# Hybrid decoder trunk on one core: where the state-space input weights are loaded and split, and when the last expert's hidden rows are turned

## The chip, the cores and the metric

One core of one Trainium2 chip runs the whole program in one launch. The metric is device time in microseconds (us), lower is better. Engines are named as in the profile: PE (TensorE matmul), PEld (its weight loads), DVE (VectorE), ACT (ScalarE), POOL (GpSimd), SP (SyncE, which only issues DMAs here).

## The reference, cut to what matters

Two layers over 512 tokens of 1024 values. Layer 0 has a mixer of sparse attention and gated linear attention, layer 1 a state-space mixer (S5); each layer ends in a norm, a mixture of 16 experts, and a second norm.

```python
for layer in range(DEPTH):                      # 2
    m = even_mixer(...) if layer % 2 == 0 else s5_mixer(h, s5_w_in, ...)
    h = layer_norm(ALPHA * h + m)
    f = hier_moe(h, ...)                        # 16 experts, 2 chosen per token
    h = layer_norm(ALPHA * h + f)

def s5_mixer(x, w_in, ...):
    u = x @ w_in                                # 512x1024 @ 1024x1024, the first thing it does
    ...
```

The change lies at the end of the experts (both layers) and, in layer 0, between there and `x @ w_in`.

## The kernel before, in words

All matmuls that need fp32 accuracy are done in three passes: an operand is split into a high part (an ACT copy to the rounded type) and a low part (a subtraction on DVE or POOL), and `mm3` (lines 103 to 108) multiplies high by high, high by low and low by high. `split` (98) makes both parts of a tile; `part` (1119 to 1126) does it for half of an expert's weight matrix.

**The experts, `Experts.run` (1279 to 1419).** An expert e has gate, up and down weights, each in two halves. PE multiplies gate, then up, then the down weights of expert e-1. The order on each engine is fixed by the code (a `manual_schedule` region with all five engines). `high()` and `low()` split the next half of the list `todo`; for e = 15 the last two of them, `(15, 4)` and `(15, 5)` (the down weights of expert 15), are split beside the up product. `hidden` (1156) applies the gate on ACT and the product on DVE; `turn_hidden` (1163) transposes the 128x512 hidden rows on PE (line 1169) and splits them into the tiles `hh` and `hl`, of which there is one buffer each. `table` (1261 to 1267) scales an expert's output on ACT and writes it to a table in DRAM (`y_d`) by a DMA that ACT issues. `fetch(i)` (1269 to 1277) is four indirect DMAs on POOL, one for each quarter of the tokens, that add rows of that table to `acc`; `fetch(1)` needs the tables up to expert 13, `fetch(0)` that of expert 14. Expert 15 goes another way: `rows` (1179) and then `combine` (1192), matmuls that place its rows, whose result DVE adds to `acc` (line 1206) once `fetch(0)` has landed.

**What is put amid the tail.** `run` gets a generator `early`. In layer 0 that is `S5.early` (1773): it loads a small table `s_gb` (the second norm's scale and shift, 2 x 1024 single values, two POOL DMAs, line 1780) and the state-space input weights `w_in`, two DMAs of 2 MB on SP's queue (line 1784), into the two `raw` buffers of the ring; this is called at e = 15, after the up product. After `fetch(0)` and `turn_hidden(15)` its second part runs `unit_in(0)` and `unit_in(1)` (1764): each splits a quarter of `w_in` in two blocks of 128x1024, ACT copy (line 100) and DVE subtraction (101). Then come the two halves of `down(15)`. In layer 1 `early` is `load_norm` (2165), two SP loads into a buffer that the last up product has to free; its later parts are empty.

**The end of the experts and the norm.** `beyond()` (1209) is a branch that is not taken here (more than 128 rows for an expert). Behind it `S5.enter` (1797) runs the norm (`closing`, 1422 to 1461) and the projection. `closing` adds each quarter (1206), squares (1435), takes the deviations, and scales quarters 0 and 1 (1459); its generator `last` does quarters 2 and 3, interleaved below, and ends in the ACT scaling at 1452. `turn(0)` transposes quarters 0 and 1 on PE (1810) and then makes for each of 8 k a high part on ACT (1815, needs `s_gb`), a difference on DVE (1817, four buffers in turn), and the low part on POOL (1819). `project((0, 1), a)` then multiplies units 0 (columns 0 to 255 of `w_in`), after that `turn(2)`, `project((2, 3), a)` with unit 1, and both again for the other half of the tokens. In this region the hand-written order holds for PE, DVE and ACT; POOL's instructions are placed by the program's own scheduler.

**What follows in `S5.mix`.** `rt.load()` (`Router.load`, 792 to 802) issues nine small POOL DMAs for the next router (`r1R`, lines 796 and 798, four of the latter; `r1rb`, 799 and 800; `r1gb`, 802 twice), and `prepare` (808) multiplies two of them on POOL. They are written behind `enter`, but POOL is not in a hand-written order there, and the scheduler puts them first behind the branch. `load_glu(0)` is 16 SP loads of 128 KB into the first `raw` buffer (line 1938), ahead of all other SP loads of the mixer, and has to wait until `unit_in(1)` has read that buffer. `put_u` (1847), `block_in(4)`, `states` and the rest follow.

Of the kernel before, what the change touches and what calls it, by code (L numbers as in the profile page):

```python
# [10 lines left out]
F32 = mybir.dt.float32  # L11
F32R = mybir.dt.float32r
# [9 lines left out]
P = 128  # L22
D = 1024
KO = D // P
# [25 lines left out]
class Ctx:  # L50
# [44 lines left out]
        self.n += 1  # L95
        return self.ring.tile([P, 4096], dt, tag="raw", name=f"raw{self.n}")[:, :n]

    def split(self, hi, lo, src):

        self.nc.scalar.activation(hi, src, AF.Copy)  # L100
        self.nc.vector.tensor_sub(lo, src, hi.bitcast(F32))  # L101

    def mm3(self, out, a, b, start, stop):

# [950 lines left out]
class Bank:  # L1055
# [17 lines left out]
    def next(self, *s):  # L1073
        self.n += 1
        return self.pair(self.pairs[(self.n - 1) % len(self.pairs)], *s)


class Experts:
# [83 lines left out]

    def turn_hidden(self, name, s):
        c = self.c
        hh = self.late.tile([P, 4, P], F32R, tag="hh", name=f"{name}hh")
        hl = self.late.tile([P, 4, P], F32R, tag="hl", name=f"{name}hl")
        ps = c.psum().rearrange("p (b t) -> p b t", b=4)
        for f in range(4):
            c.nc.tensor.transpose(ps[:, f], s.rearrange("p (q f) -> p f q", f=4)[:, f], c.ident)
        c.split(hh, hl, ps)  # L1170
        return hh, hl

    def down(self, py, h, w, half):
        for f in range(2):
            for i in range(2):
                self.c.mm3(py[i], [t[:, 2 * half + f] for t in h],
                           [t[:, i * 512:(i + 1) * 512] for t in w[f]], half + f == 0, half == 1 and f == 1)
# [101 lines left out]
    def run(self, early):  # L1279
# [34 lines left out]
        def low():  # L1314

            if lows:
                lows.pop(0)()
                load(lows.pop(0) + 6)
# [4 lines left out]
        with c.tc.manual_schedule(engines={c.nc.tensor.engine, c.nc.scalar.engine, c.nc.vector.engine,  # L1323
                                       c.nc.gpsimd.engine, c.nc.sync.engine}):
            load(0, 1)
            x = self.first_rows()
            tokens, gates = rt.slots(0, 2)
            tokens()
            nc.gpsimd.dma_start(rt.y_d[0:1, :], self.xe[0][0:1, :])
            xs = {1: gather(1)}  # L1330
            rt.early_gates()
            nc.scalar.preload_act_table(AF.Silu)
            def product(ps, raw, ks, x=x):
                for k in ks:
                    nc.tensor.matmul(ps, x[:, k], raw[:, k], start=(k == 0), stop=(k == KO - 1))  # L1335
            pg, pu = c.psum(), c.psum()
            product(pg, raws[0, 0], range(KO))
            load(2, 3)
            for _ in range(2):
                high()  # L1340
                low()
            product(pu, raws[0, 1], range(7))
            rt.gates()
            gates()
            tokens, gates = rt.slots(2, 2)
            product(pu, raws[0, 1], range(7, KO))
            load(4, 5)
            high()
            low()
            s, mul = self.hidden(f"{n}0", pg, pu)  # L1350
            mul()
            x = self.turn(f"{n}1", xs[1], [t[:, :KO] for t in self.bank.pair(2, 2 * KO, P)])
            tokens()
            xs[2] = gather(2)
            h = self.turn_hidden(f"{n}0", s)
            gates()
            high()
            low()
            self.table_rows()
            py = [c.psum(), c.psum()]  # L1360
            for i in range(2):
                self.down(py, h, parts[0, 4 + i], i)
            high()
            self.table(0, py, rt.gcol[:, 0:1])
            low()
            high()
            low()
            h = None

            def down(e, i, h):  # L1370
                if not i:
                    py[:] = [c.psum(), c.psum()]
                self.down(py, h, parts[e, 4 + i], i)
                if i and e < TABLE:
                    self.table(e, py, rt.gcol[:, e:e + 1])
                elif i:
                    ys[e] = self.rows(f"{n}{e}", py, rt.idxf[:, e:e + 1], rt.gcol[:, e:e + 1])
            for e in range(1, 16):
                pg, pu = c.psum(), c.psum()

                high()
                self.product(pg, x, parts[e, 0], 0)
                if e > 1:
                    h = self.turn_hidden(f"{n}{e - 1}", s)
                low()
                high()
                self.product(pg, x, parts[e, 1], 1)
                more = rt.slots(e + 2, 2) if e < 14 and e % 2 == 0 else ()
                low()
                s, mul = self.hidden(f"{n}{e}", pg, pu)  # L1390
                if e == 15:
                    self.fetch(1)
                for i in range(2):
                    if e > 1:
                        high()
                    self.product(pu, x, parts[e, 2 + i], i)
                    if e > 1:
                        low()
                mul()
                if e + 1 < 16:  # L1400
                    x = self.turn(f"{n}{e + 1}", xs[e + 1])
                for step in more:
                    step()
                if e + 2 < 16:
                    xs[e + 2] = gather(e + 2)
                if e == 15:
                    next(early)
                for i in range(2):
                    high()
                    if e > 1:  # L1410
                        down(e - 1, i, h)
                    low()
            self.fetch(0)
            h = self.turn_hidden(f"{n}15", s)
            next(early)
            for i in range(2):
                down(15, i, h)
        self.beyond()
        return lambda *args: self.combine([ys[15]], *args), self.xe

# [330 lines left out]
class S5:  # L1751
# [9 lines left out]
        h, l = self.bank.pair(3 + i, 4, L)  # L1761
        return [(h[:, k], l[:, k]) for k in range(4)]

    def unit_in(self, i):

        w = self.w[i] = self.bank.pair(1 + i % 2, KO, 256)
        src = self.raw[i // 2][:, :, i % 2 * 256:i % 2 * 256 + 256]
        for b in range(2):
            cols = slice(b * P, (b + 1) * P)
            self.c.split(*[t[:, :, cols].rearrange("p k (c g) -> p k c g", c=16) for t in w],  # L1770
                         src[:, :, cols].rearrange("p k (g c) -> p k c g", c=16))

    def early(self):

        c, nc = self.c, self.c.nc
        self.bank = self.get_bank()
        self.gb = self.bank.pool.tile([P, 2, KO], F32, name="s_gb")
        with nc.allow_non_contiguous_dma(reason="2048 values"):
            for i, v in enumerate((self.fn_g, self.fn_b)):
                nc.gpsimd.dma_start(self.gb[:, i], v.rearrange("(k p) -> p k", p=P))  # L1780
        self.raw, self.w = [], {}
        for i in range(2):
            t = c.raw(KO * 512).rearrange("p (k n) -> p k n", k=KO)
            nc.sync.dma_start(t, self.w_in.rearrange("(k p) n -> p k n", p=P)[:, :, i * 512:(i + 1) * 512])
            self.raw.append(t)
        yield
        self.unit_in(0)
        self.unit_in(1)
        yield

    def project(self, bs, ts, ps, ks=range(KO)):
        for k in ks:
# [4 lines left out]
    def enter(self, es, combine, free):  # L1797

        c, nc, acc = self.c, self.c.nc, self.c.acc
        with c.tc.manual_schedule(engines={nc.tensor.engine, nc.vector.engine, nc.scalar.engine}):  # L1800
            steps = closing(c, c.scope(es, "n0"), combine, free[0])
            x = self.x = self.half(0) + self.half(1)
            g, b = self.gb[:, 0], self.gb[:, 1]

# [20 lines left out]
                pass  # L1825
            ps = self.first = [c.psum() for _ in range(4)]
            self.project((0, 1), a, ps)
            b_ = turn(2)
            self.project((2, 3), a, ps)
            self.project((0, 1), b_, ps)  # L1830
# [293 lines left out]
def trunk(ctx: ExitStack, tc: tile.TileContext, x, rel_bias, ab_w_in, gla_gate_w2, gla_gate_b, gla_norm_g,  # L2124
# [3 lines left out]
    c = Ctx(tc, ctx)  # L2128
    nc = c.nc
# [4 lines left out]
    def moe(layer, mixer, early, last):  # L2134
        nonlocal bank
        es = ExitStack()
        rt = Router(c, es, ln_mix_g[layer], ln_mix_b[layer], moe_r_coarse[layer], moe_rb_coarse[layer],
                    moe_r_fine[layer], moe_rb_fine[layer], f"r{layer}")
        experts = Experts(c, rt, (moe_w_gate[layer], moe_w_up[layer], moe_w_down[layer]), f"e{layer}")
        mixer(rt, experts)  # L2140
        bank = bank or Bank(c, bank_s)
        experts.open(es, bank)
        last(es, *experts.run(early()))

    def first(rt, experts):
        su = ExitStack()
# [18 lines left out]
    def load_norm():  # L2165
        t = bank.tile(2, 2, D, dt=F32)
        for i, v in enumerate((ln_ffn_g[1], ln_ffn_b[1])):
            nc.sync.dma_start(t[:, i], bcast_row(v))
        fgb.append(t)
        yield  # L2170
        yield

    def finish(es, combine, free):
        pool, acc, (fg, fb) = c.scope(es, "n1"), c.acc, (fgb[0][:, i] for i in range(2))
# [92 lines left out]
```

## Time and profile before

| | us |
|---|---|
| three timed runs | 1344.14, 1324.39, 1338.56 (median 1338.56) |
| the profiled execution, its own time | 1330.89 |
| its span in the profile, first to last instruction | 1328.8 |
| outside the span (difference) | 2.1 |
| PE busy | 1195.4 (90%) |
| DVE busy | 1035.4 (78%) |
| ACT busy | 724.6 (55%) |
| POOL busy | 572.4 (43%) |

Times in rows are counted from the span's start. A timeline row gives start, duration, engine, line, operation, output and inputs, and in brackets how long the engine stood idle just before it and what ended that. "ACTq" and "SPq" are an engine's DMA issues. The granted clock of TensorE is given as a share of full speed.

### The profile page before, as it was taken

To read this page: it belongs to the slowest core of one execution; us is meant where nothing else is said; L and a number is where in the kernel's file an instruction comes from. 1 tells how busy PE (TensorE), PEld (TensorE's weight loads), DVE (VectorE), ACT (ScalarE), POOL (GpSimd) and SP (SyncE) were. 2 spreads that over 40 slices of the span, in tenths; PEclk is the share of its full clock that TensorE was granted. 3 is DMA by queue.
4 is the path that set the end of the run, shared out by engine and by line. 5 is a ranking of instruction groups with operands and counts; after the bars stand their busy time and mean duration, and the time that the engine had idled before them with its cause. 6 is when DMAs were issued, how large, how long until landed. Compare 5 with 4: busy or idle time off the path is not lost.

```text
span 1328.8 us, 18794 instructions
## 1 busy us (share of the span) xinstructions
PE 1195.4 (90%) x6879; PEld 954.8 (72%) x6879; DVE 1035.4 (78%) x1621; ACT 724.6 (55%) x854; POOL 572.4 (43%) x570
## 2 busy tenths in 40 slices
PE   7898798989989999999984999999988999999981
PEld 5577675567757778788864877888857787877860
DVE  5868868777578999999975567363668999999956
ACT  3443214545547777888853422332246787877842
POOL 4076934697512454455444100250002553454533
PEclk9998898999899999999996999999999999999995
DMA  9324352342379999999995788534149999999974
GB/s 229 99 74 146 108 175 73 96 133 77 110 290 333 359 382 393 359 378 409 396 281 107 219 277 267 159 127 159 48 186 338 359 394 365 383 358 405 382 213 123
DMA packets 130063, 324.56 MB, mean 244 GB/s; under 512 B 43851, under 2 KB 80995, under 8 KB 104233
## 3 DMA queue, kind: packets, MB, share of 16 engines
q1 hardware_dynamic: 106128, 285.69, 59.5%
q0 software_dynamic: 7328, 16.51, 5.3%
q10 hardware_dynamic: 16504, 21.04, 4.4%
q8 instruction: 59, 0.97, 0.3%
q14 instruction: 44, 0.35, 0.1%
HBM read 293.18 MB, written 43.49 MB: 253 GB/s over the span
## 4 chain that ended last, share of the span: by engine, by line
PE 36%; DVE 16%; DMA 14%; issue 6%; ACT 3%; POOL 1%; ACTq 0%; DVEq 0%; POOLq 0%; SPq 0%
PE ps L106 9%; DVE b L1124 9%; PE ps L107 9%; PE ps L108 9%; DMA e1xe<-r1h_d,r1idx 3%; DMA acc<-r0y_d,e0row 2%; DMA e0xe<-r0h_d,r0idx 2%; DMA acc<-r1y_d,e1row 2%; PE ps L1915 2%; ACT b L1123 2%; DMA rawd<-in_moe_w_gate_dram 2%; PE ps L167 1%; PE ps L1912 1%; PE ps L1335 1%; PE ps L940 1%
## 5 line engine op out<-in xcount | busy, mean ns | idle before, releaser
L1124 DVE TENSOR_TENSOR b<-raw,b 128x2048 fp32r<-128x2048 f32 x120 | 296.6, 2501 | 8.1 <-ACT b L1123 8.1
L1124 POOL TENSOR_TENSOR b<-rawd,b 128x2048 fp32r<-128x2048 f32 x28 | 168.4, 6015 | 204.0 <-ACT b L1123 154.8
L1123 ACT ACTIVATE b<-raw 128x2048 fp32r<-128x2048 f32 x120 | 229.7, 1918 | 35.3 <-PE ps L108 15.7
L1124 DVE TENSOR_TENSOR b<-rawd,b 128x2048 fp32r<-128x2048 f32 x36 | 160.8, 4473 | 24.0 <-ACT b L1123 23.6
L1123 ACT ACTIVATE b<-rawd 128x2048 fp32r<-128x2048 f32 x64 | 122.2, 1915 | 16.5 <-PE ps L108 7.9
L1130 POOL DMA_INDIRECT e1xe<-r1h_d,r1idx x15 | 39.5, 2636 | 64.1 <-DVE r1gcol L1051 34.7
L101 DVE TENSOR_TENSOR b<-raw,b 128x2048 fp32r<-128x2048 f32 (+1 forms) x18 | 41.3, 2312 | 32.9 <-ACT b L100 32.9
L1130 POOL DMA_INDIRECT e0xe<-r0h_d,r0idx x15 | 39.6, 2641 | 55.8 <-DVE r0gcol L1051 30.5
L107 PE MATMUL ps<-b,b 128*128 128x512 f32 (+1 forms) x160 | 56.9, 355 | 4.6 <-POOL b L1819 4.6
L106 PE MATMUL ps<-b,b 128*128 128x512 f32 (+1 forms) x160 | 57.4, 359 | 0.0
L108 PE MATMUL ps<-b,b 128*128 128x512 f32 (+1 forms) x160 | 56.7, 354 | 0.0
L106 PE MATMUL ps<-gh,b 128*128 128x512 f32 x128 | 51.2, 400 | 0.0
L107 PE MATMUL ps<-gl,b 128*128 128x512 f32 x128 | 50.1, 391 | 0.1
L108 PE MATMUL ps<-gh,b 128*128 128x512 f32 x128 | 49.8, 389 | 0.0
L603 ACT ACTIVATE lt<-lt,rmin 128x128 f32<-128x128 f32 (+3 forms) x32 | 17.9, 561 | 42.9 <-DVE rmin L601 42.9
L100 ACT ACTIVATE b<-raw 128x2048 fp32r<-128x2048 f32 (+1 forms) x18 | 34.5, 1946 | 7.2 <-DMA raw<-in_s_w_out_dram 3.7
L1864 POOL COPY s_r<-s_si 128x256 f32<-128x256 f32 x8 | 5.8, 730 | 74.2 <-DVE s_Z L1897 51.6
L107 PEld LDWEIGHTS ps<-b,b 128*128 128x128 f32 x160 | 31.5, 197 | 8.5 <-POOL b L1819 4.8
L106 PEld LDWEIGHTS ps<-b,b 128*128 128x128 f32 x160 | 31.4, 196 | 4.5 <-ACT b L1815 0.4
L108 PEld LDWEIGHTS ps<-b,b 128*128 128x128 f32 x160 | 31.4, 196 | 3.9
L670 PE MATMUL ps<-raw,oB 128*128 128x512 f32 x64 | 32.3, 629 | 0.0
L2019 POOL TENSOR_TENSOR acc<-acc,s_fg 128x1024 f32<-128x1024 f32 x4 | 12.9, 3236 | 39.6 <-DMA s_fg<-in_ln_ffn_g_dram 39.6
(1266 smaller groups left out, 3749.8 us busy)
## 6 DMA issues: line engine op xcount, KB each, us to landing
raw<-in_moe_w_up_dram SPq DMA_DIRECT2D x64, 1024.0 KB
rawd<-in_moe_w_gate_dram SPq DMA_DIRECT2D x56, 1024.0 KB
raw<-in_moe_w_down_dram SPq DMA_DIRECT2D x56, 1024.0 KB
raw<-in_moe_w_gate_dram SPq DMA_DIRECT2D x8, 1024.0 KB
rawd<-in_moe_w_down_dram SPq DMA_DIRECT2D x8, 1024.0 KB
raw<-in_s_glu_w_dram SPq DMA_DIRECT2D x64, 128.0 KB
b<-store SPq DMA_DIRECT2D x8, 1024.0 KB
s_si<-store SPq DMA_DIRECT2D x8, 770.0 KB
```

The costliest lines, as they stand in the source:

```text
L100: self.nc.scalar.activation(hi, src, AF.Copy)
L101: self.nc.vector.tensor_sub(lo, src, hi.bitcast(F32))
L106: mm(out, a[0], b[0], start=start, stop=False)
L107: mm(out, a[0], b[1], start=False, stop=False)
L108: mm(out, a[1], b[0], start=False, stop=stop)
L167: c.nc.tensor.transpose(ps[:, b], src[:, (b0 + b) * P:(b0 + b + 1) * P], c.ident)
L603: nc.scalar.activation(lt[:, :n], lt[:, :n], AF.Exp, scale=-1.0, bias=m, accum_out=self.rsum[:, h:h + 1])
L670: nc.tensor.matmul(ps, oB[:, k, tb * P:(tb + 1) * P], raw_o[1][:, k, hs], start=(k == 0), stop=(k == 3))
L1123: c.nc.scalar.activation(h, r, AF.Copy)
L1124: low = lambda: (eng or c.nc.vector).tensor_sub(l, r, h.bitcast(F32))
L1130: self.c.nc.gpsimd.indirect_dma_start(out=x, out_offset=None, in_=self.rt.h_d[:, :], in_offset=bass.IndirectOffsetOnAxis(ap=idx, axis=0), ...
L1915: nc.tensor.matmul(ps[h, j, 1:64], cw[r, i, j, h], X[b][r, i, j, 0:63], start=False, stop=True, skip_group_check=True)
```

## The change

1. `S5.early` is no generator any more and is called once, behind `fetch(0)`. It loads `w_in` on POOL's queue instead of SP's, ahead of the two `s_gb` loads. In layer 1 `load_norm` is called there too; it stays on SP.
2. `unit_in(0)` moves behind `closing` in `enter`; the subtraction of its first block goes to POOL, that of its second stays on DVE. `unit_in(1)` moves behind the first `project((0, 1), a)`.
3. POOL is put into the hand-written order of `enter`.
4. At e = 15, in both layers, the splits `(15, 4)` and `(15, 5)` move from beside the up product to beside `down(14)`, and `turn_hidden(15)` moves between the two halves of `down(14)`. `hh` and `hl` get two buffers each.

```diff
-    def split(self, hi, lo, src):
+    def split(self, hi, lo, src, engine=None):
         self.nc.scalar.activation(hi, src, AF.Copy)
-        self.nc.vector.tensor_sub(lo, src, hi.bitcast(F32))
+        (engine or self.nc.vector).tensor_sub(lo, src, hi.bitcast(F32))
...
-        hh = self.late.tile([P, 4, P], F32R, tag="hh", name=f"{name}hh")
-        hl = self.late.tile([P, 4, P], F32R, tag="hl", name=f"{name}hl")
+        hh = self.late.tile([P, 4, P], F32R, tag="hh", name=f"{name}hh", bufs=2)
+        hl = self.late.tile([P, 4, P], F32R, tag="hl", name=f"{name}hl", bufs=2)
...
                 for i in range(2):
-                    if e > 1:
+                    if 1 < e < 15:
                         high()
                     self.product(pu, x, parts[e, 2 + i], i)
...
-                if e == 15:
-                    next(early)
                 for i in range(2):
                     high()
                     if e > 1:
                         down(e - 1, i, h)
                     low()
+                    if e == 15 and not i:
+                        last = self.turn_hidden(f"{n}15", s)
             self.fetch(0)
-            h = self.turn_hidden(f"{n}15", s)
-            next(early)
+            early()
             for i in range(2):
-                down(15, i, h)
+                down(15, i, last)
...
-    def unit_in(self, i):
+    def unit_in(self, i, engines=None):
...
-                         src[:, :, cols].rearrange("p k (g c) -> p k c g", c=16))
+                         src[:, :, cols].rearrange("p k (g c) -> p k c g", c=16), engines and engines[b])
     def early(self):
         c, nc = self.c, self.c.nc
         self.bank = self.get_bank()
+        self.raw, self.w = [], {}
+        for i in range(2):
+            t = c.raw(KO * 512).rearrange("p (k n) -> p k n", k=KO)
+            nc.gpsimd.dma_start(t, self.w_in.rearrange("(k p) n -> p k n", p=P)[:, :, i * 512:(i + 1) * 512])
+            self.raw.append(t)
         self.gb = self.bank.pool.tile([P, 2, KO], F32, name="s_gb")
...
-        self.raw, self.w = [], {}
-        for i in range(2):
-            t = c.raw(KO * 512).rearrange("p (k n) -> p k n", k=KO)
-            nc.sync.dma_start(t, self.w_in.rearrange("(k p) n -> p k n", p=P)[:, :, i * 512:(i + 1) * 512])
-            self.raw.append(t)
-        yield
-        self.unit_in(0)
-        self.unit_in(1)
-        yield
...
-        with c.tc.manual_schedule(engines={nc.tensor.engine, nc.vector.engine, nc.scalar.engine}):
+        with c.tc.manual_schedule(engines={nc.tensor.engine, nc.vector.engine, nc.scalar.engine, nc.gpsimd.engine}):
             steps = closing(c, c.scope(es, "n0"), combine, free[0])
+            self.unit_in(0, (nc.gpsimd, nc.vector))
...
             self.project((0, 1), a, ps)
+            self.unit_in(1)
             b_ = turn(2)
...
-        last(es, *experts.run(early()))
+        last(es, *experts.run(early))
...
             nc.sync.dma_start(t[:, i], bcast_row(v))
         fgb.append(t)
-        yield
-        yield
```

## Rows read from the trace of the kernel before

**Rows 1.** Busy time in five stretches: columns as in the second line.
```profile
core 0: us, PE busy (x) PEld busy (x) DVE busy (x) ACT busy (x) POOL busy (x), PEclk, DMA share, GB/s
671.00:674.00 3.00, 3.00 (x15) 2.49 (x14) 3.00 (x2) 2.25 (x2) 3.00 (x1) 1.00 1.00 377
691.00:701.00 10.00, 6.41 (x16) 4.80 (x16) 1.70 (x3) 0.00 (x0) 7.64 (x5) 0.66 1.06 215
711.50:720.30 8.80, 4.08 (x17) 3.48 (x18) 5.53 (x24) 4.88 (x10) 4.68 (x15) 0.69 0.77 139
720.30:730.00 9.70, 9.70 (x63) 9.70 (x64) 3.48 (x12) 2.42 (x3) 3.97 (x7) 0.73 0.00 0
748.00:960.00 212.00, 211.21 (x1764) 170.51 (x1764) 126.08 (x194) 64.26 (x70) 34.34 (x25) 1.00 0.54 175
```

**Rows 2.** Timeline of PE, layer 0, from the first projection on.
```profile
720.30 0.58 PE L107 MATMUL ps<-b,b 128*128 128x256 f32 x1 [4.63 <-POOL b L1819]
...
728.34 1.91 PE L1810 MATMUL ps<-ident,acc 128*128 128x128 f32 x16
730.00 0.36 PE L106 MATMUL ps<-b,b 128*128 128x256 f32 x1
```

**Rows 3.** Timeline of POOL, layer 0, end of the experts to the projection.
```profile
653.74 5.77 POOL L1124 TENSOR_TENSOR b<-rawd,b 128x2048 fp32r<-128x2048 f32 x1 [9.03 <-ACT b L1123]
670.86 3.49 POOL L1274 DMA_INDIRECT acc<-r0y_d,e0row  x1 [11.35 <-DMA r0y_d<-e013y]
...
691.02 1.94 POOL L1274 DMA_INDIRECT acc<-r0y_d,e0row  x1 [8.52 <-DMA r0y_d<-e014y]
...
698.11 1.46 POOL L796 DMA_DIRECT2D r1R<-in_moe_r_coarse_dram  x1
701.38 0.94 POOL L798 DMA_DIRECT2D r1R<-in_moe_r_fine_dram  x1 [1.81 <-DMA acc<-r0y_d,e0row]
...
710.14 0.88 POOL L798 DMA_DIRECT2D r1R<-in_moe_r_fine_dram  x1 [1.68 <-DMA acc<-r0y_d,e0row]
...
713.24 0.89 POOL L802 DMA_DIRECT2D r1gb<-in_ln_mix_b_dram  x1
...
718.63 1.05 POOL L808 TENSOR_TENSOR r1R<-r1R,r1gb 128x160 f32<-128x160 f32 x2 [4.04 <-DMA r1gb<-in_ln_mix_b_dram]
719.63 4.63 POOL L1819 TENSOR_TENSOR b<-e0xe,s_gb 128x256 fp32r<-128x256 f32 x8
```

**Rows 4.** Timeline of DVE, layer 0, same stretch.
```profile
683.45 7.54 DVE L101 TENSOR_TENSOR b<-raw,b 128x1024 fp32r<-128x1024 f32 x4 [1.18 <-ACT b L100]
...
701.26 0.69 DVE L1206 CUSTOM_DVE_ANT_0 acc<-acc,ps 128x512 f32<-128x512 f32 x1 [8.56 <-DMA acc<-r0y_d,e0row]
...
707.05 0.69 DVE L1206 CUSTOM_DVE_ANT_0 acc<-acc,ps 128x512 f32<-128x512 f32 x1 [1.31 <-DMA acc<-r0y_d,e0row]
```

**Rows 5.** Timeline of ACT and its DMA issues, layer 0, same stretch.
```profile
663.69 0.33 ACTq L1267 DMA_DIRECT2D r0y_d<-e013y  x1
...
680.52 0.33 ACTq L1267 DMA_DIRECT2D r0y_d<-e014y  x1
...
681.45 7.63 ACT L100 ACTIVATE b<-raw 128x1024 fp32r<-128x1024 f32 x4
...
723.75 2.37 ACT L1452 ACTIVATE acc<-acc,cl,cl 128x1024 f32<-128x1024 f32 x2 [4.22 <-DVE cl L1451]
```

**Rows 6.** Groups by line and shape, 700 to 760 us: busy, mean ns, idle before.
```profile
L1815 ACT ACTIVATE b<-ps,s_gb 128x256 fp32r<-128x256 f32 x16 | 7.6, 573 | 8.6 <-PE ps L1810 8.6
L1817 DVE SCALAR_TENSOR_TENSOR e0xe<-ps,s_gb,b 128x256 f32<-128x256 f32 x16 | 7.4, 480 | 10.1 <-ACT b L1815 9.5 <-POOL b L1819 0.6
```

**Rows 7.** Timelines of ACT, POOL and DVE, layer 1, the same step.
```profile
1282.25 0.33 ACTq L1267 DMA_DIRECT2D r1y_d<-e114y  x1
...
1292.24 1.55 POOL L1274 DMA_INDIRECT acc<-r1y_d,e1row  x1 [9.79 <-SPq L1220]
...
1307.60 0.69 DVE L1206 CUSTOM_DVE_ANT_0 acc<-acc,ps 128x512 f32<-128x512 f32 x1 [0.93 <-DMA acc<-r1y_d,e1row]
```

## The prediction

> **What bounds the kernel now.** I read the page first, then the busy time by stretches, then the timelines of the engines around the end of layer 0's experts. The stretches show where an edit can be worth something. From 748 to 960 PE is busy 211.2 of 212 us, and from 720.30 to 730.00 all of the time, while from 711.5 to 720.3 it works 4.1 of 8.8 us [rows 1]. So everything behind 720.30 hangs on PE, and what moves PE's first real matmul there moves the rest of the layer one for one. PE's own row names its last wait: 4.63 us for the first low part that POOL makes (L1819) [rows 2].
>
> Followed back, POOL was late because L808 stood ahead of L1819 and waited 4.04 us for the small load r1gb, which POOL had issued at 713.24 [rows 3]. Those router loads were late in their turn. The four L798 loads start at 701.38 and up to 710.14, each ended by a fetch "acc": the first 0.12 us after DVE's add of the first quarter at 701.26, which waits for that fetch too [rows 3, 4]. Counted in POOL's order, each L798 load waits for the transfer that POOL issued five transfers earlier (before: the four parts of the last fetch). I carry this pattern over to the new order.
>
> The last fetch itself starts at 691.02, when expert 14's table has been written; that write was issued at 680.52, so it took 10.50 us, and the fetch landed only at 710.14, 19.12 us after its start [rows 3, 5]. In layer 1 the same fetch took 15.36 us (1292.24 to 1307.60) with no weight loads beside it [rows 7]. So layer 0 pays 3.8 us for the loads beside its fetch.
>
> **The change part by part.**
>
> *The tail of the experts (both layers).* PE gets the four transposes of expert 15 ahead of the second half of down(14), and ACT gets the split of hh and one 128x2048 high part ahead of table(14). By the new order of ACT the table's write is issued about 1.0 us later (the estimate: half a us on PE for the transposes, then ACT ends the high part shortly after PE is done). down(15) and rows(15) come some 4 us earlier, since the eight 128x1024 halves (7.63 us on ACT, 7.54 on DVE [rows 4, 5]) no longer stand between. That buys nothing by itself: DVE's adds wait for the fetch, not for PE (8.56 us before the first add [rows 4]).
>
> *The write of table 14, layer 0.* No w_in load runs beside it now. It took 10.50 us with them; expert 13's write took 7.17 us (663.69 to 670.86 [rows 3, 5]) amid the last weight loads. I take 6.5, bounds 5 and 10.5. Issued at 681.5, it lands at 688.0, and the fetch starts there, 3.0 us earlier than before.
>
> *The fetch, layer 0.* With nothing beside it I take layer 1's 15.36 us: it lands at 703.4 instead of 710.1.
>
> *The weights on POOL's queue.* They stand behind the fetch on one queue. No row shows a plain 2 MB load there. Bounds by the rows: 377 GB/s while SP loaded w_in at 671 to 674, and 215 GB/s in the stretch with the fetch [rows 1]. I take 377, since the operation is the same: 4.19 MB take 11.1 us, so the first half lands at 709.0, the second at 714.5; at 215 the second lands at 722.9. The two s_gb loads are now behind them; I give them 2 us (estimate from the small loads' spacing), so s_gb lands at 716.5. The Trainium skill ("DMA: Bandwidth & Descriptors", section "Anatomy of one DMA — SWDGE (gpsimd) path") gives a transfer there a fixed 2.0 us and 436 GB/s, estimated 9.6 us for the data of both. By that the sum below would be 1.5 us smaller. No run here shows it yet.
>
> *The router loads.* They were first behind the branch on POOL, and nothing in the change makes anything else on POOL ready sooner, so I keep them first. By the five-back pattern the four L798 loads now wait for the two w_in loads and the two s_gb loads: the last starts at 716.5 instead of 710.14. From the last L798 to the end of the last L802 POOL took 4.0 us (710.14 to 714.13 [rows 3]), so it is free at 720.5, with the memsets 721.2.
>
> *unit_in(0) behind the norm.* ACT's two copies cost 1.9 us each (7.63/4 [rows 5]) and run at 709 to 713, in time. POOL's subtraction of 128x1024 costs about 2.9 us (half of 5.77 for 128x2048 [rows 3]) and has to wait in POOL's order: 721.2 to 724.1. Only then comes L1819. Its first result (0.58 us, 4.63/8 [rows 3]) is there at 724.7, where PE starts: 4.4 us later than 720.30. ACT's L1815 needs s_gb at 716.5, DVE's L1817 follows; both are done for the first four k, then wait for POOL.
>
> *unit_in(1) behind the first projection.* Before, ACT's L1452 began 4.1 us after POOL's first L1819 (719.63 to 723.75 [rows 3, 5]) and ran 2.37. Now 724.1 + 4.1 + 2.4 = 730.6; two copies end at 734.4, and DVE's second subtraction (1.9 us, 7.54/4 [rows 4]) at 736.3. PE: the first projection took 8.04 us (720.30 to 728.34) and the transposes 1.66 (to 730.00) [rows 2], so it is ready at 724.7 + 9.7 = 734.4 and waits 1.9 us for unit 1. It goes on at 736.3 against 730.00: 6.3 us later.
>
> *load_glu(0).* Its 16 loads on SP waited for the raw buffer until 691; now until 736.3, with all of the mixer's other SP loads behind them. Nothing on DMA ran from 720.3 to 730 (0 GB/s [rows 1]), and PE has some 17 us of projections left there, so I cost it at nothing; if that cover is gone, PE's wait for the states' tables is the price, 0 to 5 us.
>
> *Layer 1.* load_norm is freed by the same product as before and costs nothing. The table's write goes out up to 1.0 us later; the fetch starts when it lands (1282.25 to 1292.24 before [rows 7]). The DMA queues were full then, so I take 0.6.
>
> Sum: 6.3 + 0.6 = 6.9 us. Against the profiled execution that is 1330.9 + 6.9 = 1337.8. That execution lies 7.7 under the median of the three runs and 3.6 under the mean of all four (1334.5). For a median of new runs I take the mean: 1334.5 + 6.9 = 1341.4, said as 1341.
>
> **The rivals.**
>
> A. *POOL puts L808 ahead of the subtraction too.* For: it stood ahead of L1819 before [rows 3]. Then r1gb, issued at 719.6, lands 5.4 us later (713.24 to 718.63), L808 takes 1.05, the subtraction ends at 729.0, PE starts at 729.6, and unit 1 (one 4.9 us later as well) lets it on at 741.2: 11.2 us in layer 0, 1346 in all. Against: the new order gives the subtraction a place of its own, and L808 needs all router loads.
>
> B. *The subtraction comes ahead of the router loads.* This is the case that is not slower. Then POOL starts it when ACT's first copy is done, at 711, and ends at 714. PE's start is set by s_gb: 716.5 + 0.57 + 0.48 [rows 6] + 0.58 = 718.1, 2.2 us sooner; unit 1 is ready at 717.6 + 4.1 + 2.4 + 3.8 + 1.9 = 729.8 against PE at 727.8, so PE goes on 0.2 us sooner than before. With layer 1: 1335. If w_in also comes faster than 377 GB/s, each us of it counts, some 2 us in all. It decides from the point where the subtraction starts ahead of 715. Against it: the router loads need nothing but the branch, and they were first there.
>
> C. *The plain loads on POOL's queue run no faster than the stretch with the fetch.* At 215 GB/s all behind them is 8.4 us later: 1350. For: nothing shows that queue faster. Against: the fetch adds to memory, these loads only write.
>
> **How the numbers follow.** Forecast 0.45, A 0.25, B 0.17, C 0.08, 0.05 for something else of either sign. Two per cent of the median is 26.8 us, about what a measurement of this kernel can tell from no change; none of the cases reaches it: 1341 lies 0.2% above the median of before and 0.5% above its mean. So "within 2%" gets 0.93, slower 0.05 (C and A together, with an SP wait), faster 0.02. The range takes in B less the three us that the runs leave open in a median, and C with as much above: 1328 to 1354. The forecast's own range, by the write's 5 to 10.5 us and s_gb's 1 to 4, is 1336 to 1348.
>
> **What would show it.** Right: the fetch starts near 688 and is landed near 703; the L798 loads end their waits on w_in and s_gb, not on "acc"; POOL's subtraction (L101) comes behind L802; PE's idle time before the first projection ends at 723 to 727, and a second wait of 1 to 3 us for DVE or ACT of L100/L101 stands before the second projection; the 212 us behind shift without a new wait; layer 1's last add moves by under 1.2 us. Wrong: POOL's L101 stands before L796 (B), or behind L808 (A); w_in takes over 18 us from the fetch's landing (C); PE waits anew in the mixer for the states' tables or for U.

## The result and the profile after

The changed kernel takes 1350.47 us (median of 20 runs) against 1338.03 of the kernel before (20 runs beside it): 1.0105 times as long, 95% interval 1.0067 to 1.0142. That is 12.4 us by the medians and some 14 by the ratio: slower, and within 2%. The forecast was 1341 with "within 2%" likeliest. The side and the range hold; the size is about twice the 6.9 us of the sum.

The two profiled executions must not be subtracted as they stand (spans 1328.8 and 1347.8): expert 15 of layer 0 already begins 8.5 us later in the second, and ahead of that point the order of instructions is the same on every engine, but for the load of `w_in`, which SP issues 1.0 us ahead of it in the kernel before. That start moves from execution to execution: in e1_tail, which lost no time, it lies at 684.05. So all times below are counted from one row, ACT's silu of expert 15, and the stage S runs from there to the silu of layer 1's expert 0. Timeline of ACT, kernel before:

```profile
668.92 0.60 ACT L1160 ACTIVATE e015s<-ps 128x512 f32<-128x512 f32 x1 [0.35 <-PE ps L108]
...
741.48 0.59 ACT L1849 COPY s_u<-ps 128x512 f32<-128x512 f32 x1 [7.76 <-POOL s_r L1865]
742.10 0.38 ACTq L1850 DMA_DIRECT2D u_d<-s_u  x1
...
993.55 0.58 ACT L1160 ACTIVATE e10s<-ps 128x512 f32<-128x512 f32 x1
```

Timeline of ACT, changed kernel:

```profile
677.43 0.60 ACT L1160 ACTIVATE e015s<-ps 128x512 f32<-128x512 f32 x1 [0.35 <-PE ps L108]
...
689.66 0.33 ACTq L1267 DMA_DIRECT2D r0y_d<-e014y  x1
...
719.71 3.75 ACT L100 ACTIVATE b<-raw 128x1024 fp32r<-128x1024 f32 x2 [4.91 <-DMA raw<-in_s_w_in_dram]
...
726.02 0.56 ACT L1812 ACTIVATE b<-ps,s_gb 128x256 fp32r<-128x256 f32 x1 [2.56 <-DMA s_gb<-in_ln_ffn_b_dram]
...
738.08 3.81 ACT L100 ACTIVATE b<-raw 128x1024 fp32r<-128x1024 f32 x2
...
754.79 0.59 ACT L1847 COPY s_u<-ps 128x512 f32<-128x512 f32 x1 [8.60 <-PE ps L108]
755.40 0.40 ACTq L1848 DMA_DIRECT2D u_d<-s_u  x1
...
1013.09 0.58 ACT L1160 ACTIVATE e10s<-ps 128x512 f32<-128x512 f32 x1
```

S is 324.63 before and 335.66 after: 11.0 us, nearly the whole loss. The copy at 754.79 (`put_u`, the first result of the projection; 741.48 in the kernel before) splits it. It comes 77.36 us behind the silu, from 72.56; from there to the end of S it is 258.30, from 252.07. So 4.8 us are lost ahead of the projection's first result and 6.2 in the mixer behind it. The two parts repeat less well than their sum: by the second profiles of both kernels (first two rows of the table below) they are 7.0 and 5.5, by the means 5.9 and 5.9.

POOL's timeline of the changed kernel answers to [rows 3]:

```profile
699.05 1.55 POOL L1274 DMA_INDIRECT acc<-r0y_d,e0row  x1 [9.93 <-SPq L1220]
...
705.64 2.48 POOL L1780 DMA_DIRECT2D raw<-in_s_w_in_dram  x2
709.02 0.89 POOL L1785 DMA_DIRECT2D s_gb<-in_ln_ffn_g_dram  x1 [0.89 <-DMA acc<-r0y_d,e0row]
712.07 0.88 POOL L1785 DMA_DIRECT2D s_gb<-in_ln_ffn_b_dram  x1 [2.17 <-DMA acc<-r0y_d,e0row]
721.77 2.85 POOL L101 TENSOR_TENSOR b<-raw,b 128x1024 fp32r<-128x1024 f32 x1 [8.81 <-ACT b L100]
724.57 0.89 POOL L796 DMA_DIRECT2D r1R<-in_moe_r_coarse_dram  x1
725.45 3.52 POOL L798 DMA_DIRECT2D r1R<-in_moe_r_fine_dram  x4
728.98 0.63 POOL L1816 TENSOR_TENSOR b<-e0xe,s_gb 128x256 fp32r<-128x256 f32 x1
```

The subtraction of unit 0 stands ahead of the router loads, and these stand between it and the first addition of the norm (L1819 before, L1816 now). DVE's adds show when the fetched quarters are there, as in [rows 4]; timeline of DVE, changed kernel:

```profile
705.66 0.69 DVE L1206 CUSTOM_DVE_ANT_0 acc<-acc,ps 128x512 f32<-128x512 f32 x1 [9.93 <-DMA acc<-r0y_d,e0row]
...
711.92 0.69 DVE L1206 CUSTOM_DVE_ANT_0 acc<-acc,ps 128x512 f32<-128x512 f32 x1 [1.50 <-DMA acc<-r0y_d,e0row]
...
1326.42 0.69 DVE L1206 CUSTOM_DVE_ANT_0 acc<-acc,ps 128x512 f32<-128x512 f32 x1 [0.96 <-DMA acc<-r1y_d,e1row]
```

The last row is the last quarter in layer 1 [rows 7].

Timeline of PE, changed kernel, which answers to [rows 2]: each bracket is a wait of the engine that sets the end.

```profile
716.06 1.33 PE L1807 MATMUL ps<-ident,acc 128*128 128x128 f32 x5 [10.77 <-DVE acc L1458]
...
726.64 0.58 PE L106 MATMUL ps<-b,b 128*128 128x256 f32 x1 [6.90 <-ACT b L1812]
...
729.67 0.58 PE L107 MATMUL ps<-b,b 128*128 128x256 f32 x1 [2.44 <-POOL b L1816]
...
732.25 0.58 PE L107 MATMUL ps<-b,b 128*128 128x256 f32 x1 [0.94 <-POOL b L1816]
...
742.05 0.38 PE L108 MATMUL ps<-b,b 128*128 128x256 f32 x1 [1.19 <-DVE b L101]
...
743.88 0.39 PE L108 MATMUL ps<-b,b 128*128 128x256 f32 x1 [1.22 <-DVE b L101]
...
770.84 1.98 PE L1882 MATMUL ps<-s_U,s_si 128*64 128x64 f32 x32 [4.55 <-DMA s_U<-u_d]
```

The first six rows are the transposes and the projection; the last is new: a wait of 4.55 us for U (the projection's result, written to DRAM and read back) in the mixer, where PE had less than 1 us of idle time in all [rows 1]. In the kernel before, the same 32 matmuls came without a wait (timeline of PE):

```profile
752.92 1.15 PE L1884 MATMUL ps<-s_U,s_si 128*64 128x64 f32 x32
```

The timeline of SP's queue in the changed kernel shows what it waits for:

```profile
743.91 10.69 SPq L1936 DMA_DIRECT2D raw<-in_s_glu_w_dram  x16
754.96 0.35 SPq L1859 DMA_DIRECT2D s_si<-store  x1
...
767.30 4.85 SPq L1853 DMA_DIRECT2D s_U<-u_d  x3
```

The same queue in the kernel before:

```profile
691.01 25.90 SPq L1938 DMA_DIRECT2D raw<-in_s_glu_w_dram  x16
...
748.49 4.63 SPq L1855 DMA_DIRECT2D s_U<-u_d  x3
```

And the busy time by stretches, changed kernel, shows the loads of `w_in` (713 to 721) and what the wait leaves behind (the last two rows):

```profile
core 0: us, PE busy (x) PEld busy (x) DVE busy (x) ACT busy (x) POOL busy (x), PEclk, DMA share, GB/s
...
713.00:717.00 4.00, 0.94 (x5) 0.94 (x6) 3.96 (x24) 1.24 (x2) 0.00 (x0) 0.50 1.02 401
717.00:721.00 4.00, 2.74 (x13) 2.33 (x11) 1.16 (x5) 1.29 (x1) 0.00 (x0) 0.50 1.03 388
...
754.79:774.79 20.00, 15.45 (x112) 13.68 (x111) 7.37 (x4) 10.50 (x9) 1.29 (x2) 0.87 0.91 292
774.79:794.79 20.00, 20.00 (x250) 15.70 (x249) 14.61 (x29) 4.94 (x6) 1.50 (x4) 0.96 0.81 244
```

The GLU loads go out from 743.91 (from 691.01 before). The write of the projection's first result is issued at 755.40, beside them and the tables, and SP reads it back at 767.30, 11.9 us later (6.4 before, 742.10 to 748.49). PE has run out of work at 766.29 and goes on at 770.84, when U has landed.

### The profile page after: what moved, and what is told of

Read it like the earlier page. It is cut to its first block, busy times and chain, and to the rows that moved or that the text cites. A ratio compares the mean times of both kernels' runs of the same rounds, so it can differ in the third digit from the quotient of the medians.

```text
span 1347.8 us, 18797 instructions
## 1 busy us (share of the span) xinstructions
PE 1194.4 (89%) x6879; PEld 957.0 (71%) x6879; DVE 1037.5 (77%) x1620; ACT 723.6 (54%) x854; POOL 574.2 (43%) x573
## 5 line engine op out<-in xcount | busy, mean ns | idle before, releaser
L1124 DVE TENSOR_TENSOR b<-raw,b 128x2048 fp32r<-128x2048 f32 x120 | 292.3, 2465 | 9.7 <-ACT b L1123 9.7
L1124 DVE TENSOR_TENSOR b<-rawd,b 128x2048 fp32r<-128x2048 f32 x36 | 151.6, 4214 | 31.1 <-ACT b L1123 31.0
L101 DVE TENSOR_TENSOR b<-raw,b 128x2048 fp32r<-128x2048 f32 (+1 forms) x17 | 41.0, 2422 | 48.4 <-ACT b L100 48.4
L590 DVE TENSOR_TENSOR lt<-sc,toep 128x256 f32<-128x256 f32 x24 | 31.2, 1299 | 8.5 <-PE ps L167 8.4
```

The source lines that it names most:

```text
L101: (engine or self.nc.vector).tensor_sub(lo, src, hi.bitcast(F32))
L590: nc.vector.tensor_add(bm[:, n - near:n], sel[tb][:, n - near:n], toep[:, h, 256 - near:])
L1124: low = lambda: (eng or c.nc.vector).tensor_sub(l, r, h.bitcast(F32))
```

## The experiments

Three theories stood against each other: the loss is in the tail; it is in the late loads of `w_in` and `s_gb`; it is in the late unit 1 and what hangs on it (the GLU loads, SP's queue). In the table are, by the rows above, when `put_u` comes behind the silu, and S less that.

| kernel | put_u | S less put_u | S | ratio to the kernel before |
|---|---|---|---|---|
| before, two profiles | 72.56, 70.95 | 252.07, 253.86 | 324.63, 324.81 | 1 |
| changed, two profiles | 77.36, 77.96 | 258.30, 259.38 | 335.66, 337.34 | 1.0105 (1.0067 to 1.0142) |
| e1_tail, e10_tail | 71.16, 72.09 | 252.24, 253.18 | 323.40, 325.27 | 0.9946 (0.9885 to 1.0006), 0.9959 (0.9917 to 1.0002) |
| e2_s5 | 77.07 | 259.27 | 336.34 | 1.0102 (1.0041 to 1.0164) |
| e3_sp | 74.08 | 255.14 | 329.22 | one run, no ratio |
| e4_glu | 78.29 | 259.56 | 337.85 | one run, no ratio |
| e5_gb | 76.08 | 259.05 | 335.13 | one run, no ratio |
| e6_r1 | 66.87 | 275.46 | 342.33 | 1.0179 (0.9958 to 1.04) |
| e7_u1 | 76.16 | 253.11 | 329.27 | 1.0018 (0.9973 to 1.0063) |
| e8_gb | 68.47 | 254.08 | 322.55 | 1.002 (0.997 to 1.0071) |
| e9_both | 66.07 | 264.64 | 330.71 | 1.0073 (1.0011 to 1.0134) |

**Both kernels again.** 

> The kernel before once more, to see how far two profiles of one program differ. Measured by two stretches of the trace: stretch S, from the gate activation of expert 15 of layer 0 to that of expert 0 of layer 1 (324.6 us in the first profile of before, 335.7 in that of the changed kernel), and stretch T, from the gate activation of expert 15 of layer 1 to the end of the span (58.2 and 58.6). If the loss lies in the change, S here is 324.6 within 2 us and T 58.2 within 0.5, and only what stands ahead of S differs. If the 11 us are a difference between executions, S here may come out anywhere up to 336.

> The changed kernel once more. If the loss lies in the change, S is 335.7 within 2 us, with PE waits of about 6.9 us for L1812, 3.4 for L1816, 2.4 for the split of unit 1 and 4.5 us for the states' U. If it is a difference between executions, S may be near 325.

Measured: the second values in the first two rows of the table. S repeats within 0.2 us before and 1.7 after (its two parts only within 1.8), while the spans (1323.9 and 1359.0) differ from the first pair by 5 and 11. S is the measure that a single profile can carry.

**The two halves of the change.** e1_tail has only part 4 of the change (splits, `turn_hidden(15)`, two buffers), e2_s5 only parts 1 to 3.

The lines in which they differ from the kernel before (e1_tail has these, e2_s5 all the others of the diff):

```diff
-                    if e > 1:
+                    if 1 < e < 15:
                         high()
...
+                    if e == 15 and not i:
+                        last = self.turn_hidden(f"{n}15", s)
             self.fetch(0)
-            h = self.turn_hidden(f"{n}15", s)
```

> The kernel before with part 4 of the change alone: the last two halves are split beside down(14), the hidden rows of expert 15 turn between its halves, two buffers for hh and hl; the weights are loaded on SP and taken apart as before. Theory (the tail costs only a later table write, about 0.6 us a layer; the loss is in the S5 parts): S 325 to 326, T 58.2 to 58.8, ratio 1.000 to 1.001. Rival (the tail carries the loss, since the table's write sets the fetch): S 328 or more.

> The changed kernel without part 4: loads on POOL behind the last fetch, unit 0 behind the norm, unit 1 behind the first projection, POOL in the fixed order; the tail of the experts as before. Theory: S 334 to 336, T 58.2, ratio 1.007 to 1.010, with the wait for U of 3 to 5 us still there. Rival (the tail carries the loss): S 325 to 328.

Measured: S 323.40 with the tail alone, 336.34 with the state-space parts alone; the ratio of e2_s5, 1.0102, is that of the whole change. The loss is in parts 1 to 3. The tail costs nothing that these runs show; whether it gains is taken up below.

**The loads back where they were.** e3_sp is the changed kernel with `early()` called beside `down(14)` again and `w_in` on SP's queue; the splits stay late.

```diff
+                if e == 15:
+                    early()
...
             self.fetch(0)
-            early()
...
-            nc.gpsimd.dma_start(t, self.w_in...)
+            nc.sync.dma_start(t, self.w_in...)
```

> The changed kernel with w_in back on SP's queue and all loads at the old place (behind the up product of expert 15); units 0 and 1 stay behind the norm and the first projection. In this build POOL does the router loads and L808 first, then the subtraction of unit 0. S is 324.7 in the kernel before and 336.4 in the changed one (means of two and three profiles). Theory (late weights and late s_gb cost about half, late unit 1 and the late GLU loads the rest): PE's wait for L1812 falls under 2 us, a wait for POOL of some 6 us comes in its place, unit 1 still costs 2, U still 4 to 5; S 330 to 333. Rival (the queue of the loads does not matter, only the late taking apart): S 335 or more.

PE's waits in e3_sp (line numbers are one higher than in the changed kernel), 690 to 980 us; columns: us in total, times, longest:

```profile
PE ps L107 <- POOL b L1817: 5.2, 1, 5.2
PE ps L1883 <- DMA s_U<-u_d: 3.9, 1, 3.9
...
PE ps L108 <- DVE b L101: 1.6, 2, 1.2
```

The 6.90 us for ACT's first high part, which stands behind its copies of `w_in` and needs `s_gb`, are gone and `put_u` comes 3.3 us sooner, with a wait for POOL such as the kernel before had. (POOL's order changes with it: here the router loads and L808 stand ahead of the subtraction, as the prediction had it.) The waits for unit 1 and for U stay, 0.8 and 0.6 us shorter: in the main they do not belong to the late loads. The part behind `put_u` is 3.2 us shorter too, more than these waits explain; with one profile, and parts that repeat within 1.8 us, that is left open. This parts the loss in two.

**One late thing at a time.** e4_glu moves `load_glu(0)` behind the projection's `put_u` loop; e5_gb loads `s_gb` ahead of `w_in`, both still behind the fetch (two blocks of `early` change places; the lines here are e4_glu's).

```diff
e4_glu
-            for _ in load_glu(0):
-                pass
             for b in range(2):
...
                     self.unit_in(2 + b // 2)
+            for _ in load_glu(0):
+                pass
```

> The changed kernel with the 16 GLU loads of the mixer issued behind the fetches of the states' tables and of U, not ahead of them. Theory (the GLU loads, held back until unit 1 is done, fill the queues and make the write and fetch of U late): PE's wait for U falls from 4.5 to 5.4 us to under 1, U's write lands in 6 to 8 us instead of 12, and S falls by 5 to 331 to 332. Rival (U is late because the projections are late): the wait for U stays above 3 and S at 335 or more.

> The changed kernel with the two s_gb loads issued ahead of the two w_in loads. Theory: ACT's L1812 no longer waits for s_gb (2.56 us in the changed kernel) but only for its two copies of unit 0, so PE starts 2 to 3 us sooner and S is 333 to 334.5. Rival (POOL's subtraction and the router loads ahead of L1816 set PE's start): S stays within 1 us of 336.

e4_glu missed: S 337.85. Its waits say why:

```profile
PE ps L106 <- ACT b L1812: 6.9, 1, 6.9
...
PE ps L1882 <- DMA s_si<-store: 4.3, 1, 4.3
```

The wait for U is gone, as expected (the states of block 0 run 11.4 us behind `put_u`, as in the kernel before, from 16.0), but 24 GLU loads in a row, 16.84 us of SP's queue, now stand ahead of a later `s_si` (a table of the states), and PE waits 4.3 us for that one. The wait was moved, not removed. e5_gb missed too (S 335.13): it gains 1.3 us at `put_u`, less than ACT's wait of 2.56 us for `s_gb` promises: `w_in` is now behind `s_gb` (ACT's first copy of it comes 43.5 us behind the silu, from 42.3), and PE's wait for POOL's L1816 grows from 3.4 to 4.5 us. The first addition stands ahead of the router loads here, but it waits 2.20 us for DVE, whose own subtraction of unit 0 comes first; the router loads stand between the later additions.

**Unit 1 early.** e7_u1 is the changed kernel with one line moved.

```diff
             self.unit_in(0, (nc.gpsimd, nc.vector))
+            self.unit_in(1)
...
             self.project((0, 1), a, ps)
-            self.unit_in(1)
             b_ = turn(2)
```

> The changed kernel with unit_in(1) issued right behind unit_in(0), ahead of the norm, in place of behind the first projection. Measure S: from the silu of layer 0's expert 15 to that of layer 1's expert 0 (changed kernel 335.7 and 337.3, kernel before 324.6 and 324.8). Theory 1 (the late unit 1 costs twice: PE waits 2.4 us for its low half, and the GLU weights, which need its buffer free, hold SP's queue and the transfer engines so that the states wait 4.5 to 5.4 us for their input): both waits go, the first s_gb activation starts about 1.2 us later because ScalarE now casts unit 1 first; S falls by 5.7 to 6.6 to 329.5 to 331. Theory 2 (the w_in and s_gb transfers behind the fetch are the whole loss, and the waits behind them only move, as one did when the GLU loads alone were moved): S stays at 335 to 338. Time by theory 1 about 6 us under the changed kernel's.

PE's waits in e7_u1, same stretch and columns:

```profile
PE ps L1808 <- DVE acc L1458: 10.0, 1, 10.0
PE ps L106 <- ACT b L1813: 8.2, 1, 8.2
...
PE ps L107 <- POOL b L1817: 3.9, 2, 2.9
```

The waits for unit 1 and for U are both gone. The one for ACT's first high part is 1.3 us longer, since ACT makes all four copies of units 0 and 1 ahead of it (7.42 us) and `s_gb` is there by then; S is 329.27. The GLU loads start 51.5 us behind the silu in place of 66.5. The ratio falls to 1.0018. So the place of one line is 6 to 8 us of the loss, most of it in the mixer. What is left, 4.6 us, lies ahead of `put_u` (76.16 against 72.56 and 70.95), where the late loads and the splits behind them stand; e3_sp, with the loads early, took 3.3 us off that part.

**The wait that was there before.** [rows 2] show 4.63 us for POOL, and the prediction read it as L808 waiting for `r1gb`. e6_r1 is the kernel before with the two multiplications of L808 on DVE for this router; e8_gb is e1_tail with `r1gb` loaded on SP behind the tables.

> The kernel before with the two multiplications of L808 for the second router done on DVE, in the mixer's fixed order there, so that POOL's L1819 does not stand behind them. Theory (PE's wait of 4.6 to 5.6 us for L1819 is what the stretch before the projection costs, one for one): that wait falls under 1 us, S is 320 to 321, ratio 0.996 to 0.998. Rival (the wait is hidden by what follows, such as U): S stays within 1 us of 324.7.

> The kernel before with the tail change alone (e1_tail) and router 1's two norm rows (r1gb) fetched on SP's queue behind the mixer's tables in place of last on GpSimd's: GpSimd's two multiplications of line 808 wait for those rows and stand ahead of the norm's additions that the first projection waits 4.6 us for; in this kernel they stand behind them. Theory 1 (the wait in e1_tail is that of the multiplications for the rows): PE's wait for GpSimd ahead of the first projection falls from 4.6 to 1 to 2 us, the first put_u comes 3 to 4 us earlier behind expert 15's silu (67 to 68, from 71.2), S falls from 323.4 to 319.5 to 321, and the time to 0.989 to 0.994 of the kernel before. Theory 2 (what was saved is waited for again: for the states' tables behind the rows' transfers, or for the multiplications ahead of the router): put_u is earlier and S stays at 322 to 326.

The reading holds: `put_u` comes at 66.87 and 68.47, at least 4 and 2.7 us sooner than in the kernels that they are built on, PE's wait for POOL falls to 1.4 and 0.7. Both missed in S all the same (342.33 and 322.55), and neither kernel is shown to be faster. In e6_r1 DVE reaches L808 only at 884.73, in its hand-written order, and PE stands idle for 20.51 us ahead of the router's matmul, which reads the product. Timeline of DVE, e6_r1:

```profile
884.73 4.83 DVE L808 TENSOR_TENSOR r1R<-r1R,r1gb 128x160 f32<-128x160 f32 x2
```

Timeline of PE, e6_r1:

```profile
889.67 3.60 PE L811 MATMUL ps<-r1R,ones 128*128 128x40 f32 x16 [20.51 <-issue]
```

In e8_gb S is 322.55, 0.9 and 2.7 under the two profiles with the tail alone, and the ratio of 1.002 shows no gain: the part behind `put_u` is 0.9 to 1.8 us longer, no more than such a part differs between two profiles of one kernel. There PE waits 1.2 us for the states' `s_A`, and the granted clock of the 20 us from there on is 0.91, where e1_tail has 1.00.

**The GLU loads away from the fetch.** e9_both is e8_gb with the first GLU half loaded in steps between the mixer's blocks.

```diff
-            for _ in load_glu(0):
-                pass
...
-            more = load_glu(1)
+            more = (k for i in range(2) for k in load_glu(i))
```

> e8_gb with one more edit: the first GLU half is no longer loaded on SP while expert 15's fetch runs, but in steps between the mixer's blocks, ahead of the second half (load_glu(0) and load_glu(1) as one sequence, eight steps in blocks 4 and 5, eight in 6 and 7). Theory 1 (the 2 MB of GLU loads beside the fetch, not the w_in loads ahead of it, are what made the fetch of the kernel before longer than the changed kernel's): the adds of the fetched quarters come 3 to 4 us earlier behind expert 15's silu (last one at 39 to 40, from 43.2), put_u at 64.5 to 66 from 68.5, S at 318.5 to 320.5 from 322.6, the time 3 us under e8_gb's, near 0.993 of the kernel before. Theory 2 (the fetch is limited by itself): the last add stays at 42 to 43 and S at 322 to 324. Theory 3 (the loads are missed or collide later, as in e4_glu): the adds come earlier and S rises above 323, with a wait of PE for s_si or for a GLU unit in the mixer.

The last quarter's add comes 40.5 us behind the silu, from 43.2, and `put_u` 2.4 us sooner: the 2 MB of GLU loads beside the fetch are what lengthened it. But S rises by 8.2, in the mixer. Busy time of the stretch from 40 to 80 us behind `put_u` (columns as in the fence of stretches above), kernel e8_gb:

```profile
794.68:834.68 40.00, 40.00 (x581) 30.89 (x577) 30.74 (x55) 12.34 (x16) 3.87 (x8) 1.00 0.83 274
```

The same stretch, kernel e9_both:

```profile
796.64:836.64 40.00, 36.37 (x434) 27.75 (x434) 23.68 (x42) 11.69 (x14) 1.97 (x6) 0.82 0.91 287
```

PE is idle for 3.6 us (1.93 us for `b`, a table of the states, and 1.71 for U) and the granted clock over the stretch is 0.82: 434 matmuls in place of 581.

**The tail once more.** 

> The tail half of the change alone once more, for its time (the first timing gave 0.9946 of the kernel before, interval 0.9885 to 1.0006). Theory 1 (the trace is right: S 323.4 against 324.7 and the end of layer 1 at most 1 us earlier, some 2 us in all): 0.997 to 0.9995, S at 323 to 324, put_u at 70.5 to 72 behind the silu of expert 15. Theory 2 (the first timing is right and the tail is worth 7 us that the two stages do not show): 0.994 to 0.996.

Two timings, 0.9946 and 0.9959, both with an interval that just touches 1. S in the second profile is 325.27, so no stage of the trace shows a gain of that size. Nor does the pair that differs by the tail alone: without it (e2_s5) the ratio is 1.0102, with it (the whole change) 1.0105. A gain of some half a per cent is possible and not shown; no other version here has a lower ratio.

## Why the prediction was right, and where its steps failed

*The side.* Right, and only in part for the reason given. PE does get new waits ahead of the projection, and all behind hangs on PE. But the largest term of the sum, 4.4 us for a subtraction that comes behind the router loads, did not come as described: PE's start moved by 0.9 us. The 3.5 us that this term had too much made up for part of the 5.5 to 6.2 us in the mixer, which stood in the sum at nothing. That the total came out so near is in part luck. Two of the prediction's own signs of being wrong are in the trace: POOL's L101 stands ahead of L796, and PE waits anew for U.

*The tail.* The table's write goes out 0.63 us later by the silu (12.23 against 11.60; predicted 1.0). Layer 1 shows the rest. Counted from its silu of expert 15, the fetch starts 0.2 us later and the last add, at 1326.42 now, 0.24 us (predicted 0.6).

*The write of table 14.* This term failed. It takes 9.39 us (689.66 to 699.05), inside the bounds but not 6.5, so the fetch starts 0.5 us sooner, not 3.0. The `w_in` loads beside it are only some 1 us of its time: without them it takes 8.8 to 10.1 us (changed kernel, two profiles, e2_s5, e4_glu, e5_gb, e7_u1), with them 10.1 to 10.5 (kernel before, two profiles, both runs of the tail alone, e3_sp, e8_gb, e9_both). The prediction's own rows had the better measure: the same write in layer 1, with no such load, took 9.99 us (1282.25 to 1292.24 [rows 7]). From 689 to 693, with the fetch of the earlier tables beside the write and no weight load, the busy share of the transfer engines is 1.06 at 200 GB/s; that this fetch is what makes the write slow is not shown.

*The fetch.* Right. Its third quarter is added 12.87 us behind its start, from 16.03; layer 1 shows 12.9. The cause named (loads beside it) was right too; e9_both shows that these are the GLU loads, which start with the fetch (691.01), not `w_in`.

*`w_in` and `s_gb` behind the fetch.* Near. The first half is there 20.7 us behind the fetch's start (predicted 21.0), `s_gb` after 27.0 (28.5). The stretches from 713 to 721 show 401 and 388 GB/s where 377 was taken; rival C's 215 is excluded. The Trainium skill ("DMA: Bandwidth & Descriptors", section "Anatomy of one DMA — SWDGE (gpsimd) path") gives 436 GB/s: the trace is 8 to 11% below it in these two stretches.

*POOL's order.* Failed: the subtraction came ahead of the router loads, as in rival B, and L808 ahead of only the last two of the eight additions. B's time did not follow. It had PE start 2.2 us sooner; PE started 0.9 us later (52.24 behind the silu, from 51.38). Between the two (3.1 us) lie 2.5 us of the later start of the fetch, 1.5 the other way for `s_gb`, and some 1.9 us in which five router loads stand between the subtraction and the first L1816 (DVE's first difference is done at 727.1, POOL begins at 728.98). The three make 2.9. Neither the forecast nor B had the router loads there.

*Unit 1.* Predicted 1.9 us of wait, measured 2.4 (1.19 and 1.22). From PE's start to `put_u` the changed kernel takes 3.9 us longer: these waits, 0.94 more for POOL, and some 0.5 us in which the 114 matmuls ahead of `put_u` (738.72 to 754.79) keep PE busy for 13.66 us in place of 13.14, at a granted clock of 1.00 in both.

*`load_glu(0)`.* The step that cost most. The prediction said "I cost it at nothing", with 0 to 5 us as the price if the cover was gone. The cover of 17 us was counted for the tables; what was late was U, which must be written, by ACT, and read back by SP, beside and behind the GLU loads. It cost 4.55 us of wait (5.3 in the second profile), and more by the clock that PE had behind it (the last section); the part behind `put_u` is 5.5 to 6.2 us longer in all. e7_u1, where the loads start 15 us sooner, has neither the wait nor, within 1.8 us, the longer mixer. The price was in the text, on the wrong side of the sum; with 5 us there the sum is 12, close to the 11.0 to 12.5 of S, though by the errors above that closeness proves little.

*The base.* Of the 9.5 us between 1341 and 1350.47, 3.5 are the base: 1334.5 was the mean of four executions, and the median of 20 is 1338.03.

## What to carry to other kernels

A buffer that is split later frees later: whoever waits for that buffer, and all that is queued behind him, has to be followed to its first reader on the busy engine, through every write and read back on the way. Loads that were put behind a transfer on one queue landed behind all of it here, the small ones too (`s_gb` 27.0 us behind the start of the fetch). And an edit that removes a wait in one place is worth what the whole stage shows, not what the wait was: three experiments here (e4_glu, e6_r1, e9_both) took 2 to 5 us off one place and lost as much or more later in the same stage.

## What the runs showed of the hardware

A wait of PE inside a busy stretch could cost more than itself. In the changed kernel the granted clock is 1.00 from 762.00 to 766.29, where PE is busy, and 0.50 (1.2 GHz of 2.4) from 770.84, behind the wait of 4.55 us for U, to 774.84; it is 1.00 again from 776.84. The first 32 matmuls behind the wait took 1.98 us in place of 1.15. In e9_both waits of 1.71 us (to 820.33) and 1.93 us (to 823.41) lie close together, and the clock is 0.50 from 824 to 838. It is no clean law here: the second profile of the kernel before has a wait of 1.65 us (to 772.19) at 1.00 throughout (754.77 to 790), and e7_u1, with a wait of 0.50 us (to 778.97), falls to 0.56 to 0.59 from 781 to 785. What sets the fall is not shown.

Loads of 4 KB made of single values were slow in two places. On POOL's queue behind the 4 MB of `w_in` the two of `s_gb` took 13.8 and 16.5 us from issue to landing, and on SP's in e8_gb the second of `r1gb` held the queue for 5.36 us where its issue on POOL took 0.9 (timeline of SP's queue, e8_gb):

```profile
751.83 5.36 SPq L808 DMA_DIRECT2D r1gb<-in_ln_mix_b_dram  x1
```

The write of U, 256 KB, took 11.9 us to its reading back beside the GLU loads and tables, and 6.4 in the kernel before, without the GLU loads.
